# Two-layer hybrid attention trunk on one core: causal additions behind the sparse mask, block flips copied half by VectorE, two groups of turns side by side

## The chip, the cores and the metric

One NeuronCore of a Trainium2 chip runs the whole program. The metric is device time in microseconds (us). The kernel before took 1001.78 us in the median of 3 runs (1001.54 to 1001.94).

## What is computed

Two identical layers on x of 256 tokens by 1024 channels, all in float32. Each layer is half a SwiGLU feed-forward step (2816 hidden channels), a mixer, and half a feed-forward step again:

```python
h = h + 0.5 * swiglu(rms_norm(h), ffn1)
u = rms_norm(h); P = u @ w_in
# A: 4 heads, one shared key/value head; the 64 best keys per query by an 8-head ReLU indexer
# B: 4 heads, one block of 256, so plain causal attention here
# C: 8 heads, s + cumsum(log f)[q] - cumsum(log f)[k], output gated by a sigmoid
h = h + concat(o_A, o_B, o_C) @ w_out
h = h + 0.5 * swiglu(rms_norm(h), ffn2)
```

A and B have normed and rotated queries and keys, C normed ones. Logits above the diagonal are masked before the softmax.

## The kernel before

**Matrix products.** Each float32 weight is split into a high part (rounded by ScalarE, line 126) and a low part (the difference, taken by VectorE, line 130). TensorE multiplies high by high, high by low and low by high, so most of its work is products of 128x512 at line 340. The class `Weights` loads 1 MB pieces through SP's queue, five at a time, and splits them into units of 1024 columns up to seven ahead of their use; `pump` makes one high part and the low part of the unit before. `high` and `low` make one of the two alone.

**The mixer.** `mixer` goes through the columns of `w_in` in 8 chunks of 4 units. After each unit a counter `step` goes up by one (1 to 32), `run_side` emits the work that is due at that step by the numbers given to `at_step`, and one `pump` follows. A number of 28.5 is thus emitted after unit 29, 21.3 after unit 22. All engines run their instructions in the order in which they were emitted; an instruction whose input isn't ready holds up all behind it on its engine, and no other engine. So the table of step numbers sets when TensorE meets each group of small turns between its products, and nothing moves them at run time.

The pieces that the change and the prediction speak of, for each layer:

- `log_sigmoid` and `forget` make the forget logs `lf` (ScalarE, VectorE). `cumsum` turns them on TensorE (line 905, two turns) and sums them along the tokens on VectorE (line 907). `sums_out` writes the sums to DRAM, `sums_in` reads them back, spread over all partitions, into `first` (in the tile `tab`) and `later` (tiles `laterkT` and `laterlater`), 512 KB each, through SP's queue.
- `causal_part(0)` and `(1)` add the causal mask to `first` and the first `later` on GpSimd (line 932), so that the masks of the C heads are ready made. `causal_part(2)` and `(3)` do the second half on VectorE, later (`w2`, `w3` in `AC_ORDER`).
- `a_rope` rotates the sparse heads' queries `aqr` and key `ak` on GpSimd (steps 18 and 19). `a_norm` (number 21.3) sums the squares on VectorE (`ssa`), takes the roots on GpSimd (line 351) and scales the key into `akd` on GpSimd (line 720). `a_turn` (28.5) turns four blocks of `aqr` and two of `akd` on TensorE (line 970) and copies them out on ScalarE.
- GpSimd also has the roots and scalings of the C heads' keys (`y_ck`, `cka`), which stand ahead of `y_a` and `akd` in its order.
- `topk` finds the 64 best keys on VectorE (lines 883 and 884), and `amask` turns what is left into the sparse mask (line 895).
- At step 30 the text `EARLY` is emitted word by word: `S` flips the B heads' probabilities on TensorE (line 180), copies them out of PSUM (`spread`, by `turned`, line 193), and issues the A heads' scores and the B heads' values; `m` masks a head (line 1092), `e` takes its exponentials, `Q` and `q` make a high part, `j` a low part. Then units 31 and 32 follow on TensorE, and `AC_ORDER` is emitted.

PSUM has two rotating sets of four banks, `acc` and `gu`.

Of the kernel before, what the change touches and what calls it, by code (L numbers as in the profile page):

```python
# [10 lines left out]
F32 = mybir.dt.float32  # L11
# [3 lines left out]
ALU = mybir.AluOpType  # L15
# [3 lines left out]
P = 128  # L19
S = 256  # L20
# [6 lines left out]
TOPK = 64  # L27
# [10 lines left out]
WARM = 6  # L38
BRIDGE = 3
P_BUFS = 4  # L40
EARLY = "S Q q m0 e0 m1 e1 m2 e2 b0 b1 m3 j B0 B1 e3"
AC_ORDER = """
    h0 n0 d0 C n1 d1 d2 d3 T c0 F0 k0 F1 y0 y1 c1 k1 s2 v0 v1 m4 m5 g o0 o1 e4 e5 s3 s4
    h1 m6 m7 w2 e6 e7 l q q n2 n3 w3 m8 m9 h2 h3
# [1 line left out]
    r0 r1 n5 j F4 F5 y4 y5 h4 j v4 v5 o4 o5 j  # L46
    p h5 h6 h7 Z r2 N p r3 p r4 p M x2 p x3 p
"""
B_TURN, A_ROPE, B_STEP, A_ROOT, A_TURN, SUMS_STEP, TOP_STEP, A_STEP = 18, 18, 20, 21.3, 28.5, 21, 15, 30


CHUNKS = [
# [102 lines left out]
def kernel(ctx: ExitStack, tc: tile.TileContext, x, ffn1_norm, ffn1_w_gate, ffn1_w_up, ffn1_w_down,  # L155
# [10 lines left out]
    at = ctx.enter_context(tc.tile_pool(name="at", bufs=1))  # L166
# [5 lines left out]
    V, A, G, T = nc.vector, nc.scalar, nc.gpsimd, nc.tensor  # L172

    def bank(tag):
        return psum.tile([P, 512], F32, name="ps_" + tag, tag=tag)
# [6 lines left out]
    def turned(ps, dst, copies):  # L182
        for e, copy in enumerate(copies):
            d = dst[..., 64 * e:64 * e + 64]
            n = 64
            for k in d.shape[1:-1]:
                n *= k
            src = ps[e][:, :n]
            if len(d.shape) == 3:
                src = src.rearrange("p (b j) -> p b j", j=64)  # L190
            else:
                src = src.rearrange("p (a b j) -> p a b j", a=d.shape[1], j=64)
            copy(d, src)
# [4 lines left out]
    def tmp(n):  # L198
        return tp.tile([P, 512], F32, name="tmp", tag="tmp")[:, :n]
# [39 lines left out]
    W = Weights(tc, raw_pool, split_pool)  # L239
# [89 lines left out]
    causal = cp.tile([P, 3 * P], F32, name="causal")  # L329
# [12 lines left out]
    def mm3(o, lhs, rhs, start, stop):  # L342
        mm(o, lhs[0], rhs[0], start, False)
        mm(o, lhs[0], rhs[1], False, False)
        mm(o, lhs[1], rhs[0], False, stop)
# [344 lines left out]
    def mixer(l, norm, nxt):  # L690
        side, count = [], itertools.count()
        step = [0]

        def at_step(n, fn):
            side.append((n, next(count), fn))

        def run_side():
            due = sorted(x for x in side if x[0] <= step[0])
            for x in due:
                x[2]()  # L700
            side[:] = [x for x in side if x[0] > step[0]]
# [47 lines left out]
        st = {}  # L749
# [44 lines left out]
        def post_ib(ps):  # L794
# [10 lines left out]
            for t in range(2):  # L805
                x = small[t][:, None, 0:64]
# [24 lines left out]
                A.activation(la, la, AF.Ln, bias=1.0)  # L831
                A.activation(small[0][:, 0:1], ones[:, 0:1], AF.Exp)

            at_step(SUMS_STEP - 3, log_sigmoid)
            def forget():
                V.scalar_tensor_tensor(lf, fg, 0.0, la, op0=ALU.min, op1=ALU.subtract)

            at_step(SUMS_STEP - 2, forget)
            st["ikT"] = at.tile([P, 1, S], F32, name="ikT", tag="qs")

            def turn_ik():
# [42 lines left out]
                V.match_replace(out=st["score"][t], in_to_replace=m8, in_values=st["score"][t], imm_value=-3e38)  # L884

            def amask_begin():
                st["amask"] = at.tile([P, 3 * P], F32, name="amask", tag="amask")
                G.tensor_copy(st["amask"][:TOPK, 0:P], causal[:TOPK, 0:P])

            at_step(A_STEP - 4, amask_begin)  # L890

            def amask():
                am, score = st["amask"], st["score"]
                for d, x in ((am[:, P:], score[1]), (am[TOPK:, :P], score[0][TOPK:])):
                    V.tensor_scalar(d, x, -2e38, NEG, op0=ALU.is_gt, op1=ALU.mult)

            at_step(A_STEP - 0.5, amask)

            for r in range(TOPK // 8):
                at_step(TOP_STEP + 2 * r, lambda: topk(1))  # L900
# [20 lines left out]
                    nc.sync.dma_start(to, bass.AP(tensor=src.tensor, offset=src.offset + h * S,  # L921
                                                    ap=[[0, P], [S, k], [1, n]]))

            at_step(SUMS_STEP + 1, cumsum)
            at_step(SUMS_STEP + 3, sums_out)
            at_step(SUMS_STEP + 5, sums_in)
            for i in range(2):
                at_step(A_STEP - 2, lambda i=i: causal_part(i))

        def causal_part(i):  # L930
            x = st["first"][:, 2 * i:2 * i + 4] if i % 2 == 0 else st["later"][i // 2][:, :, 1]
            (V if i > 1 else G).tensor_tensor(x, x, causal[:, None, 0:P].to_broadcast([P, 4, P]), op=ALU.add)

        def post_a(ps):
            ss = sm.tile([P, 2, 5], F32, name="ssa", tag="ss")
# [116 lines left out]
        def tanh():  # L1052
            ps, hr = st.pop("cg"), st["hr"]
            sg = at.tile([P, 2, 512], F32, name="sg", tag="sg")
            for t in range(2):
                A.activation(sg[:, t], ps[t], AF.Tanh, scale=hr[:, t:t + 1])
            st["sg"] = sg
            for _ in range(2):
                bank("gu")


        def run_heads(hs, qk, emit=None):
            pj, pt, op, sums, bs, wide, flipped, gated, high = {}, {}, {}, {}, {}, {}, {}, {}, {}
            divided = range(2)
            blocks = ((slice(0, P), slice(0, P), slice(0, P)), (slice(P, 3 * P), slice(P, S), slice(0, S)))
            tag = "acc" if emit else "gu"
# [66 lines left out]
            def spread(p):  # L1133
                both = pp.tile([P, 8, P], F32, name="pT", tag="pT", bufs=2)
                kind, h = hs[2 * p]
                turned(flipped.pop(p), both[:, :6] if p in divided else both,
                       (A.copy if emit else V.tensor_copy, A.copy))
                pt[p] = [both[:, 3 * e:3 * e + 3].rearrange("p a b -> p (a b)") for e in range(2)]
                gated[p] = both[:, 6:8].rearrange("p a b -> p (a b)")
                if kind == "C":  # L1140
                    o = st["gate"][:, h // 2]
                    if p not in divided:
                        o = tmp(S)
                        G.tensor_tensor(o, gated[p], st["gate"][:, h // 2], op=ALU.mult)
                    gated[p] = o
# [36 lines left out]
            if emit is None:  # L1182
                return scores, masks, exps, roots, divide, flip, spread, values, outT
# [20 lines left out]
        def both_scores(_):  # L1204
# [8 lines left out]
            for p in range(2):  # L1213
                b_values(p, st["keys"][p][:, S:])

        todo = dict(S=both_scores, D=divide, d=lambda i: divide(i, V), s=scores, m=masks, e=exps, n=roots, F=flip, y=spread, v=values, o=outT,
                    Q=lambda _: W.high(), q=lambda _: W.high(), j=lambda _: W.low(),
                    b=lambda p: st["B"][1](p), B=lambda p: st["B"][2](p), T=lambda _: tanh(), w=causal_part)

        def do(text):  # L1220
            for word in text.split():
                todo[word[0]](int(word[1:] or 0))

        at_step(A_STEP, lambda: do(EARLY))

        oT = {}
        posts = dict(ib=post_ib, a=post_a, b=post_b, ck=post_ck, cq=post_cq, cv=post_cv, cg=post_cg)
        index_queries()
        for name, cols in CHUNKS[1:]:
            n = sum(c[1] for c in cols)  # L1230
            ps = [bank("gu") for _ in range(2)]
            for u in range(4):
                w = W.take()
                for kk in range(2):
                    k = 2 * u + kk
                    for t in range(2):
                        ts = slice(t * P, (t + 1) * P)
                        mm3(ps[t][:, :n], (norm.h[:, k, ts], norm.l[:, k, ts]), [v[:, kk] for v in w],
                            k == 0, k == KT - 1)
                step[0] += 1  # L1240
                run_side()
                if step[0] < A_STEP and step[0] != 8:
                    W.pump()
            posts[name](ps)
            if step[0] == 8:
                W.pump(2)
# [70 lines left out]
        def norm_out(_):  # L1317
# [5 lines left out]
            for t in range(2):  # L1323
# [3 lines left out]
                    p=lambda _: W.pump(), Z=residuals, N=norm_T, M=norm_out)  # L1327
# [23 lines left out]
    for l in range(DEPTH):  # L1351
        norm = ffn(norm, lambda: Norm(1, l), lambda: before_mixer(l), l == 0)
        norm = mixer(l, norm, lambda: Norm(2, l))
        norm = ffn(norm, (lambda: Norm(0, l + 1)) if l + 1 < DEPTH else None)
# [37 lines left out]
```

## Time and profile before

| | |
|---|---|
| median of 3 runs | 1001.78 us |
| the profiled execution | 1001.55 us |
| its span | 999.8 us |
| TensorE (PE) busy | 995.5 us, 100% of the span |
| its weight loads (PEld) | 856.5 us, 86% |
| VectorE (DVE) busy | 799.3 us, 80% |
| ScalarE (ACT) busy | 597.4 us, 60% |
| GpSimd (POOL) busy | 162.0 us, 16% |
| mean granted TensorE clock | 0.999 |

The span runs from the first to the last instruction; the time of a run is 1.75 us longer than the span in this execution. TensorE's instructions overlap in the profile, and their ends are modelled: what a product costs is read from the distance between the starts of two that follow each other. The two mixers lie at about 208 to 318 us and 703 to 813 us.

### The profile page before, as it was taken

How to read it: one execution, taken by the hardware profiler on the slowest of the kernel's cores; microseconds unless marked ns; L12 is line 12 of the kernel's file. 1: busy time of each engine (PE TensorE's matmuls, PEld its weight loads, DVE VectorE, ACT ScalarE, POOL GpSimd, SP SyncE). 2: the span in 40 equal slices, each digit the busy share in tenths (PEclk: the TensorE clock that was granted, in tenths of full speed). 3: DMA queues.
4: the chain of work that ended last, by engine and by line, in shares of the span. 5: the costliest groups of instructions: out<-in, count | busy, mean ns of one | idle time of the engine just before them, and what ended most of it. 6: DMA issues, size and time to landing. Idle time of an engine off the chain costs nothing.

```text
span 999.8 us, 15219 instructions
## 1 busy us (share of the span) xinstructions
PE 995.5 (100%) x5692; PEld 856.5 (86%) x5692; DVE 799.3 (80%) x1482; ACT 597.4 (60%) x1118; POOL 162.0 (16%) x188
## 2 busy tenths in 40 slices
PE   9999999999999999999999999999999999999998
PEld 8888888888878888888888888889888788888887
DVE  5978778789998777777888777787899977777775
ACT  6655555597786555555465555556968765555552
POOL 2003000058812000000000020001677210000000
PEclk9999999999999999999999999999999999999999
DMA  9865647475725555555655655565566164464731
GB/s 291 274 224 160 224 156 238 129 238 188 230 87 169 173 164 193 187 195 196 199 169 176 207 183 198 185 208 166 192 211 232 58 208 159 140 238 148 232 128 43
DMA packets 133498, 184.80 MB, mean 185 GB/s; under 512 B 7152, under 2 KB 106800, under 8 KB 133424
## 3 DMA queue, kind: packets, MB, share of 16 engines
q1 hardware_dynamic: 133392, 183.82, 56.2%
q8 instruction: 45, 0.74, 0.3%
q14 instruction: 29, 0.24, 0.1%
q10 hardware_dynamic: 32, 0.01, 0.0%
HBM read 182.75 MB, written 1.06 MB: 184 GB/s over the span
## 4 chain that ended last, share of the span: by engine, by line
PE 98%; DMA 1%; SPq 0%; ACT 0%; issue 0%; DVE 0%
PE ps_gu L340 66%; PE ps_acc L340 30%; PE ps_acc L180 1%; DMA raw<-in_ffn_w_up_dram 1%; PE ps_acc L375 1%; PE ps_gu L180 1%; SPq L100 0%; SPq L225 0%; PE ps_gu L375 0%; PE ps_acc L970 0%; ACT wh L126 0%; PE ps_acc L402 0%; PE ps_acc L844 0%; PE ps_acc L905 0%; DVE trunk L419 0%
## 5 line engine op out<-in xcount | busy, mean ns | idle before, releaser
L130 DVE TENSOR_TENSOR wl<-raw,wh 128x1024 fp32r<-128x1024 f32 (+2 forms) x342 | 421.6, 1240 | 27.1 <-ACT wh L126 27.1
L126 ACT CAST wh<-raw 128x1024 fp32r<-128x1024 f32 (+2 forms) x341 | 341.2, 1037 | 14.4 <-PE ps_acc L340 7.7
L340 PE MATMUL ps_gu<-xhl,wh 128*128 128x512 f32 (+1 forms) x1472 | 347.6, 388 | 0.2 <-ACT wh L126 0.2
L340 PEld LDWEIGHTS ps_gu<-xhl,wh 128*128 128x128 f32 x1472 | 272.5, 188 | 54.4 <-ACT wh L126 0.7
L340 PEld LDWEIGHTS ps_gu<-xhl,wl 128*128 128x128 f32 x1472 | 187.5, 191 | 4.1 <-DVE wl L521 0.2
L340 PE MATMUL ps_gu<-xhl,wl 128*128 128x256 f32 (+1 forms) x1472 | 190.3, 282 | 0.0
L484 DVE TENSOR_TENSOR tmp<-ps_gu,tmp 128x256 f32<-128x256 f32 x176 | 72.8, 422 | 109.3 <-ACT tmp L483 109.0
L340 PE MATMUL ps_acc<-wh,hh 128*128 128x512 f32 (+1 forms) x352 | 137.3, 390 | 0.0
L340 PE MATMUL ps_acc<-wl,hh 128*128 128x512 f32 (+1 forms) x352 | 137.0, 389 | 0.0
L340 PE MATMUL ps_acc<-wh,hl 128*128 128x512 f32 (+1 forms) x352 | 136.6, 388 | 0.0
L340 PE MATMUL ps_gu<-wh,xhl 128*128 128x512 f32 (+2 forms) x448 | 133.4, 375 | 0.0
L483 ACT COPY tmp<-ps_gu 128x256 f32<-128x256 f32 x176 | 63.4, 371 | 92.1 <-PE ps_gu L340 91.9
L498 ACT CAST hh<-tmp 128x256 fp32r<-128x256 f32 x80 | 32.6, 407 | 120.2 <-DVE tmp L495 120.2
L340 PEld LDWEIGHTS ps_gu<-wh,xhl 128*128 128x128 f32 x448 | 82.5, 188 | 14.1 <-issue 1.7
L490 ACT ACTIVATE tmp<-tmp 128x256 f32<-128x256 f32 x88 | 36.9, 419 | 82.7 <-DVE tmp L488 82.5
L340 PE MATMUL ps_gu<-wl,xhl 128*128 128x512 f32 (+2 forms) x224 | 83.2, 372 | 0.0
L351 POOL TENSOR_TENSOR y_n<-msq,minus_half 128x2 f32<-128x2 f32 x6 | 7.0, 1174 | 441.9 <-DVE msq L350 441.9
L340 PEld LDWEIGHTS ps_acc<-wh,hl 128*128 128x128 f32 x352 | 66.1, 188 | 13.9
L340 PEld LDWEIGHTS ps_acc<-wh,hh 128*128 128x128 f32 x352 | 66.2, 188 | 12.6
L340 PEld LDWEIGHTS ps_acc<-wl,hh 128*128 128x128 f32 x352 | 66.3, 188 | 12.3 <-DVE wl L130 0.2
L340 PEld LDWEIGHTS ps_gu<-wl,xhl 128*128 128x128 f32 x224 | 42.2, 188 | 5.9
L508 DVE TENSOR_TENSOR tmp<-tmp,rb 128x256 f32<-128x256 f32 x88 | 37.7, 428 | 3.0
(237 smaller groups left out, 901.5 us busy)
## 6 DMA issues: line engine op xcount, KB each, us to landing
raw<-in_ffn_w_down_dram SPq DMA_DIRECT2D x44, 1024.0 KB, 5.0
raw<-in_ffn_w_gate_dram SPq DMA_DIRECT2D x42, 1024.0 KB, 6.9
raw<-in_ffn_w_up_dram SPq DMA_DIRECT2D x42, 1024.0 KB, 7.8
raw<-in_w_in_dram SPq DMA_DIRECT2D x24, 1024.0 KB, 5.1
raw<-in_w_out_dram SPq DMA_DIRECT2D x8, 1024.0 KB, 5.0
raw<-in_w_in_dram SPq DMA_DIRECT2D x4, 768.0 KB, 5.0
raw<-in_w_in_dram SPq DMA_DIRECT2D x4, 656.0 KB, 4.2
raw<-in_ffn_w_gate_dram SPq DMA_DIRECT2D x3, 512.0 KB, 7.5
```

Source lines behind the costliest of these rows:

```text
L126: self.nc.scalar.copy(hv, src)
L130: (engine or self.nc.vector).tensor_tensor(lv, self.srcs[self.n_low], hv.bitcast(F32), op=ALU.subtract)
L180: T.transpose(b[:, 64 * i:64 * i + 64], src[r], ident[r, r])
L340: T.matmul(o, l, r, start=start, stop=stop, skip_group_check=True)
L351: G.tensor_tensor(y, dst, minus_half[:, :n], op=ALU.pow)
L375: T.transpose(ps[:, i, t * P:(t + 1) * P], trunk[:, t, (2 * mp + i) * P:(2 * mp + i + 1) * P], ident)
L483: A.copy(o, ps[:, 1])
L484: V.tensor_tensor(o, ps[:, 0], o, op=ALU.add)
L490: A.activation(th, t_, AF.Tanh, scale=0.5)
L498: (V.tensor_copy if late else A.copy)(hh, t_)
L508: V.tensor_tensor(t_, t_, norm.rb, op=ALU.mult)
```

## The change

Six edits, the same in both layers:

1. `A_TURN` goes from 28.5 to 24, and `SUMS_STEP` from 21 to 24 with `cumsum` at `SUMS_STEP` in place of one after it. The turns of the forget logs go from step 22 to 24, those of the sparse heads from 29 to 24, right behind them. The forget logs themselves stay at steps 18 and 19.
2. `sums_out` goes from step 24 to 26, `sums_in` from 26 to 27.
3. The mask `amask` is not emitted ahead of `EARLY` any more; it is a word `a` in it, behind `S` and a low part `j`.
4. At step 29 only a high part is made; its low part is that `j`, behind `S`.
5. `amask` has one more block of 128 columns, into which VectorE copies the causal mask behind the sparse mask. GpSimd's `causal_part(0)` and `(1)` are emitted behind it and read this block in place of `causal`.
6. `spread` copies the B heads' flips half by VectorE and half by ScalarE, in place of all by ScalarE.

```diff
-EARLY = "S Q q m0 e0 m1 e1 m2 e2 b0 b1 m3 j B0 B1 e3"
+EARLY = "S j a Q q m0 e0 m1 e1 m2 e2 b0 b1 m3 j B0 B1 e3"
...
-B_TURN, A_ROPE, B_STEP, A_ROOT, A_TURN, SUMS_STEP, TOP_STEP, A_STEP = 18, 18, 20, 21.3, 28.5, 21, 15, 30
+B_TURN, A_ROPE, B_STEP, A_ROOT, A_TURN, SUMS_STEP, TOP_STEP, A_STEP = 18, 18, 20, 21.3, 24, 24, 15, 30
...
-            at_step(SUMS_STEP - 3, log_sigmoid)
+            at_step(18, log_sigmoid)
...
-            at_step(SUMS_STEP - 2, forget)
+            at_step(19, forget)
...
-                st["amask"] = at.tile([P, 3 * P], F32, name="amask", tag="amask")
+                st["amask"] = at.tile([P, 4 * P], F32, name="amask", tag="amask")
...
-                for d, x in ((am[:, P:], score[1]), (am[TOPK:, :P], score[0][TOPK:])):
+                for d, x in ((am[:, P:3 * P], score[1]), (am[TOPK:, :P], score[0][TOPK:])):
                     V.tensor_scalar(d, x, -2e38, NEG, op0=ALU.is_gt, op1=ALU.mult)
-
-            at_step(A_STEP - 0.5, amask)
+                V.tensor_copy(am[:, 3 * P:], causal[:, 0:P])
+                for i in range(2):
+                    causal_part(i)
+
+            st["mask"] = amask
...
-            at_step(SUMS_STEP + 1, cumsum)
-            at_step(SUMS_STEP + 3, sums_out)
-            at_step(SUMS_STEP + 5, sums_in)
-            for i in range(2):
-                at_step(A_STEP - 2, lambda i=i: causal_part(i))
+            at_step(SUMS_STEP, cumsum)
+            at_step(SUMS_STEP + 2, sums_out)
+            at_step(SUMS_STEP + 3, sums_in)
...
-            (V if i > 1 else G).tensor_tensor(x, x, causal[:, None, 0:P].to_broadcast([P, 4, P]), op=ALU.add)
+            late = i > 1
+            mask = causal[:, 0:P] if late else st["amask"][:, 3 * P:]
+            (V if late else G).tensor_tensor(x, x, mask[:, None].to_broadcast([P, 4, P]), op=ALU.add)
...
-                       (A.copy if emit else V.tensor_copy, A.copy))
+                       (V.tensor_copy, A.copy))
...
-                if step[0] < A_STEP and step[0] != 8:
+                if step[0] < A_STEP - 1 and step[0] != 8:
                     W.pump()
+                if step[0] == A_STEP - 1:
+                    W.high()
```

On TensorE, in the first layer's mixer of the kernel before, the turns of the forget logs (`lf`) stand between units 22 and 23, and 84 products later those of the sparse heads between units 29 and 30:

```order
L340 MATMUL ps_gu<-wh,xhl 128x512
L905 MATMUL ps_acc<-ident,lf 8x128 x2
L340 MATMUL ps_gu<-wh,xhl 128x512
...
L340 MATMUL ps_gu<-wh,xhl 128x512
L970 MATMUL ps_acc<-ident,aqr 128x128 x4
L970 MATMUL ps_acc<-ident,akd_2514 128x128
L970 MATMUL ps_acc<-ident,akd_2515 128x128
L340 MATMUL ps_gu<-wh,xhl 128x512
```

In the changed kernel both stand together between units 24 and 25:

```order
L340 MATMUL ps_gu<-wh,xhl 128x512
L908 MATMUL ps_acc<-ident,lf 8x128 x2
L973 MATMUL ps_acc<-ident,aqr 128x128 x4
L973 MATMUL ps_acc<-ident,akd_2514 128x128
L973 MATMUL ps_acc<-ident,akd_2515 128x128
L340 MATMUL ps_gu<-wh,xhl 128x512
```

The forget logs' turns moved back by 24 products, the sparse heads' forward by 60. GpSimd's instructions up to `akd` stand in the same order in both kernels.

On VectorE, at step 30 of the first layer, the kernel before has the last low part (line 130) between the last round of `topk` and the mask:

```order
L884 MATCH_REPLACE score_2339<-m_2979,score_2339 128x256
L130 TENSOR_TENSOR wl<-raw,wh 128x1024
L895 TENSOR_SCALAR amask<-score_2339 128x256
L895 TENSOR_SCALAR amask<-score_2338 64x128
L1092 ISA tmp,nm<-ps_acc,amask,minus_a 128x128
```

and the changed kernel:

```order
L884 MATCH_REPLACE score_2339<-m_2977,score_2339 128x256
L193 COPY pT<-ps_acc 128x6x64 x2
L130 TENSOR_TENSOR wl<-raw,wh 128x1024
L895 TENSOR_SCALAR amask<-score_2339 128x256
L895 TENSOR_SCALAR amask<-score_2338 64x128
L896 COPY amask<-causal 128x128
L1095 ISA tmp,nm<-ps_acc,amask,minus_a 128x128
```

Two copies of the flips went ahead of the low part, and one copy of the causal mask went behind the sparse mask.

On SP's queue the three reads of the sums stood ahead of the first piece of the next feed-forward step's weights and now stand behind it:

```order
 L100 DMA raw<-in_w_in_dram 128x4x512 x8
-L100 DMA raw<-in_w_out_dram 128x2x1024 x3
-L911 DMA sums_of<-tmp 8x256
-L100 DMA raw<-in_w_out_dram 128x2x1024
-L921 DMA tab<-sums_of 128x8x128
-L921 DMA laterkT<-sums_of 128x1024
-L921 DMA laterlater<-sums_of 128x1024
+L100 DMA raw<-in_w_out_dram 128x2x1024 x4
+L914 DMA sums_of<-tmp 8x256
 L100 DMA raw<-in_ffn_w_gate_dram 128x8x256
+L924 DMA tab<-sums_of 128x8x128
+L924 DMA laterkT<-sums_of 128x1024
+L924 DMA laterlater<-sums_of 128x1024
```

The write of the sums now stands behind the last piece of `w_out`.

## Rows read from the trace of the kernel before

**Rows 1.** The page, busy time and share of the span, with instructions.

```profile
PE 995.5 (100%) x5692; PEld 856.5 (86%) x5692; DVE 799.3 (80%) x1482; ACT 597.4 (60%) x1118; POOL 162.0 (16%) x188
```

**Rows 2.** Waits of PE over the whole span: us in total, times, longest.

```profile
PE ps_gu L340 <- POOL minus_half L219: 1.0, 1, 1.0
PE ps_gu L340 <- ACT wh L126: 0.2, 1, 0.2
```

**Rows 3.** Timeline of PE, first mixer, steps 22 to 24: start, length, engine, what.

```profile
250.34 0.38 PE L905 MATMUL ps_acc<-ident,lf 128*8 128x128 f32 x2
250.47 0.48 PE L340 MATMUL ps_gu<-wh,xhl 128*128 128x512 f32 x1
250.79 0.39 PE L340 MATMUL ps_gu<-wl,xhl 128*128 128x512 f32 x1
...
255.80 0.61 PE L340 MATMUL ps_gu<-wh,xhl 128*128 128x512 f32 x2
```

**Rows 4.** Timeline of PE, first mixer, the sparse heads' turns at step 29.

```profile
269.63 0.60 PE L970 MATMUL ps_acc<-ident,aqr 128*128 128x128 f32 x4
270.07 0.38 PE L970 MATMUL ps_acc<-ident,akd 128*128 128x128 f32 x2
270.20 0.48 PE L340 MATMUL ps_gu<-wh,xhl 128*128 128x512 f32 x1
```

**Rows 5.** Timeline of POOL, first mixer, up to the sparse heads' key.

```profile
251.16 2.91 POOL L351 TENSOR_TENSOR y_ck<-c_ss,minus_half 128x16 f32<-128x16 f32 x1 [4.68 <-DVE c_ss L350]
...
256.20 1.95 POOL L351 TENSOR_TENSOR y_a<-ssa,minus_half 128x10 f32<-128x10 f32 x1
258.23 0.76 POOL L720 TENSOR_TENSOR akd<-ak,y_a 128x128 f32<-128x128 f32 x2
```

**Rows 6.** Timeline of DVE, first mixer, the sparse heads' sums of squares.

```profile
255.16 0.17 DVE L350 TENSOR_SCALAR ssa<-ssa 128x10 f32<-128x10 f32 x1
```

**Rows 7.** Timelines of PE and of POOL, second mixer, the same places.

```profile
745.37 0.48 PE L340 MATMUL ps_gu<-wh,xhl 128*128 128x512 f32 x1
...
753.13 0.76 POOL L720 TENSOR_TENSOR akd<-ak,y_a 128x128 f32<-128x128 f32 x2
```

**Rows 8.** Timelines of POOL, DVE, ACT and PE, first mixer, around step 30.

```profile
273.58 1.26 POOL L932 TENSOR_TENSOR tab<-tab,causal 128x512 f32<-128x512 f32 x1
...
273.85 3.32 DVE L130 TENSOR_TENSOR wl<-raw,wh 128x1024 fp32r<-128x1024 f32 x1
277.09 0.52 DVE L895 TENSOR_SCALAR amask<-score 128x256 f32<-128x256 f32 x2
280.50 1.22 DVE L130 TENSOR_TENSOR wl<-raw,wh 128x1024 fp32r<-128x1024 f32 x1
285.28 1.02 DVE L193 COPY pT<-ps_gu 128x384 f32<-128x384 f32 x2
...
275.84 1.52 PE L340 MATMUL ps_acc<-pT,vB 128*64 128x256 f32 x16
```

**Rows 9.** DMA issues (us to landing), SP's timeline, DVE's first C-head mask, first mixer.

```profile
laterlater<-sums_of SPq DMA_DIRECT2D x1, 512.0 KB, 8.1
...
268.53 0.38 SPq L100 DMA_DIRECT2D raw<-in_ffn_w_gate_dram  x1
...
286.98 0.29 DVE L1092 CUSTOM_DVE_ANT_0 tmp<-ps_gu,tab 128x128 f32<-128x128 f32 x1
```

**Rows 10.** Timeline of PE, start and end of the span; windows of the end.

```profile
1.05 2.93 PE L340 MATMUL ps_gu<-ones 128*128 128x128 f32 x12 [1.05 <-POOL minus_half L219]
4.12 1.11 PE L537 MATMUL ps_acc<-ident,trunk 128*128 128x128 f32 x4
7.50 0.60 PE L537 MATMUL ps_acc<-ident,trunk 128*128 128x128 f32 x4
996.47 0.28 PE L340 MATMUL ps_gu<-wh,hl 128*128 128x256 f32 x1
998.00:999.80 1.80, 0.00 (x0) 0.00 (x0) 0.00 (x0) 0.00 (x0) 0.00 (x0) 0.71 0.21 73
```

More of the change, by code (lines that the diff above doesn't have):

```diff
@@ L1217, in mixer @@
                     Q=lambda _: W.high(), q=lambda _: W.high(), j=lambda _: W.low(),
-                    b=lambda p: st["B"][1](p), B=lambda p: st["B"][2](p), T=lambda _: tanh(), w=causal_part)
+                    b=lambda p: st["B"][1](p), B=lambda p: st["B"][2](p), T=lambda _: tanh(), w=causal_part,
+                    a=lambda _: st["mask"]())
         def do(text):
```

## The prediction

> **What bounds the kernel now.** I read the page first: TensorE is busy for 995.5 of 999.8 us [rows 1]. The waits of PE come next: the longest is 1.0 us at the start of the program, and the other is 0.2 us [rows 2]. So no wait of a mixer is there to be removed. Busy time of overlapping products could hide small waits, so I looked at the starts. From the product that starts at 250.79 to the one at 255.80 there are 22 steps [rows 3], 5.01 / 22 = 0.228 us each, and I take the other stretches of wide products as the same. TensorE runs at its own pace through both mixers, and the kernel gets faster only by less work on TensorE. It gets slower by whatever makes TensorE wait, to the full amount, since nothing later has slack to give it back.
>
> The Trainium skill judges TensorE's headroom otherwise: Perfetto Trace Analysis, "Identifying the Most-Contended Engine", calls matmul busy time a bad measure and asks for the busy share of weight loads. That share is 86% here [rows 1], which by the rule leaves headroom, and rival 4's 999.4 us is what it could give; the even starts above say that this headroom is no waiting time, and the measurement decides.
>
> **Part 1: the turns side by side.** This is the edit that touches TensorE's order.
>
> What it saves: a group of turns between wide products costs its own time and a slower first product behind it. The forget logs' group takes 250.47 - 250.34 = 0.13 us, and the product behind it holds its place for 250.79 - 250.47 = 0.32 us in place of 0.23 [rows 3]: 0.22 us in all. The two turns themselves stay, so joining the groups saves some 0.1 us a layer.
>
> What it adds: the sparse heads' turns need `akd` from GpSimd, and they move forward past 60 products. Where does TensorE get there?
> - Behind the old stop the first product starts at 250.47, the second at 250.79, and the 24th at 255.80 [rows 3]. Unit 25's first would start at 256.03.
> - The stop at step 22 is gone, so all this comes 0.22 earlier: the forget logs' turns start at 255.81, and take 0.13.
> - The four turns of `aqr` take 270.07 - 269.63 = 0.44 [rows 4]. So TensorE asks for `akd` at 255.81 + 0.13 + 0.44 = 256.38.
>
> When is `akd` there? GpSimd gets its sums of squares from VectorE at 255.16 + 0.17 = 255.33 [rows 6], but it is still with the C heads' keys, which it began at 251.16 after waiting for VectorE, and takes the root only at 256.20. The two scalings run from 258.23 to 258.99 [rows 5]. None of what comes before on GpSimd or VectorE is moved by the change, and VectorE's order up to these sums is the same. So TensorE waits 258.99 - 256.38 = 2.6 us. In the kernel before the same turns came at 269.63, 11 us behind `akd`; that cover is what the new place gives up.
>
> Sum of one layer: I allow 0.08 us for the hand-over, as between the end of `y_a` at 258.15 and the scaling that reads it [rows 5], and 0.07 for the last `akd` turn. Unit 25 then starts at 258.99 + 0.08 + 0.07 = 259.14, 3.1 us later than before. The old stop at step 29 is not paid any more, 270.20 - 269.63 = 0.57 [rows 4]; the slower product behind a stop is paid once in both kernels, there or here. So 3.1 - 0.57 = 2.5 us. In the second mixer the product behind the old stop starts at 745.37, unit 25 would start at 750.93, and the scalings end at 753.13 + 0.76 = 753.89 [rows 7], 2.96 behind it, just as 258.99 is behind 256.03. So twice 2.5: **+5.0 us**. Bounds of one layer: 1.7 and 3.3, the 0.76 of the scalings to either side, since the scan of the sums that VectorE did beside them moves away and a low part takes its place.
>
> **Part 2: the clock.** A wait of 2.6 us has no like inside this trace. The nearest is the end: the last product starts at 996.47 and lasts 0.28, and the window from 998.00 to 999.80 has a granted clock of 0.71 [rows 10]. With levels of 1 and 0.5 this means a fall to 1.2 GHz about 0.76 us into the window, at 998.8, 2.0 us after TensorE's last work. The forecast wait is longer than these 2.0. The price is seen at the start: four turns took 1.11 us at 4.12 and 0.60 at 7.50 [rows 10], so TensorE, working from 1.05 on, was at half pace for at least 3.1 and at most 6.5 us, and lost half of it, 1.5 to 3.2. I take 1.6 for a fall, near the lower end: at the start the engine also waited between its pieces, and here wide products follow at once. One example of a fall doesn't tell whether each wait of this length brings one. I take it that one of the two layers has it: **+1.6 us**. Bounds: 0 and twice 3.2.
>
> A rule speaks against this term. The Trainium skill (TensorE: Matmul & The Clock Gate, "Why this matters for your kernels") bids to avoid only longer idle gaps than the one that I forecast, so by it the clock stays at 2.4 GHz and the time is 1006.8 us. No row here shows such a gap with work behind it. It is the first rival below.
>
> **Part 3: the rest, at nothing.**
> - GpSimd's additions behind the mask. Before, they ran from 273.58 on, 1.26 us each, and a low part on VectorE that began at 273.85 took 3.32 us where another took 1.22 [rows 8]. Some 2 us of VectorE come free. TensorE doesn't wait for VectorE there [rows 2], so the gain is spent on idle time. In their new place they run beside the sparse heads' masks; if they block VectorE again it costs as much as before. First use is at 286.98 [rows 9], 9.9 us behind the mask at 277.09.
> - The copies of the flips. VectorE pays 1.02 us for two [rows 8] and ScalarE pays as many less. TensorE's values of the B heads start at 275.84 [rows 8] and need all four. VectorE was through with its selection at 273.85, so its two end by about 274.9, 0.9 us ahead, and with TensorE 2.5 us later there is more. If that cover is gone, the cost is at most 1.0 us a layer.
> - The copy of the causal mask: at most half of the 0.52 us that VectorE takes for the two pieces of the sparse mask [rows 8], 0.26 us, which the 2 us that come free cover.
> - The low part behind `S`: the same instruction, some 1 us later. Units are split several ahead of their use, 12 products or 12 x 0.228 = 2.7 us of TensorE each, so nothing waits.
> - SP's queue: the write of the sums moves behind one weight piece, the reads behind another that was issued at 268.53; the reads took up to 8.1 us to land [rows 9]. Behind it they land by 268.9 + 8.1 = 277.0, and by 285.1 if the piece's own transfer delays them by as much again, ahead of the masks at 286.98. The weight pieces get ahead of the reads, so no weight comes later.
>
> **Sum.** Of the profiled execution: 1001.55 + 5.0 + 1.6 = 1008.15. The median of the runs stands 0.23 us above it, so I predict 1008.4 us.
>
> **The rivals.**
> 1. The wait without a fall of the clock: 1001.78 + 5.0 = 1006.8. For it: one example of a fall is little, and it came with no work behind it. Against it: that example needed only 2.0 us.
> 2. A fall in both layers: 1006.8 + 3.2 = 1010.0. For it: both waits are of one length. Against it: the same doubt.
> 3. `akd` is there in time, so only the joining counts: 1001.78 - 2 x 0.1 = 1001.6, not slower. It decides from the point at which GpSimd ends `akd` 2.6 us earlier. For it speaks only that the C heads' keys waited 4.68 us for VectorE [rows 5]; against it, nothing in the change makes VectorE earlier there.
> 4. VectorE held TensorE in a way that the waits don't show, and its 2 us a layer free TensorE: the 2.1 us less the 1.0 of the copies, twice, give 1001.6 - 2.2 = 999.4, if there is also no wait for `akd`. Against it are the even starts [rows 3].
> 5. A longer wait, because GpSimd's order is disturbed or PSUM's next bank is still read by VectorE's mask of a B head: 1 us more a layer, 1010.4 with a fall in one.
>
> **How the numbers follow.** Wait with one fall 0.40, without 0.27, with two 0.20, longer 0.06; `akd` in time 0.05, VectorE freed 0.02. The range reaches from the case without a fall, with its wait 0.5 us a layer shorter, to the case with two falls, with 0.2 us a layer more: 1005.8 to 1010.4. It leaves out rivals 3 and 4 and the outer part of the bounds. A measurement of this kernel can tell about 0.2%, 2 us, from no change. Slower by more than that: 0.93. Within it: 0.05. Faster: 0.02.
>
> **What would show it.** Right: in the waits of PE, two of about 2.6 us at the turns of `akd`, on GpSimd's scaling; a granted clock below 1 in the window behind one of them, with wide products 0.45 apart; VectorE's low part at step 30 back at 1.2 us. Part 1 is wrong if TensorE goes through these turns without a wait, or for another input; part 2 if the clock stays at 1, or falls in both layers. Part 3 is wrong if TensorE waits for a flip's copy, a mask or a low part behind step 30. The whole is wrong if the time is under 1004.

## The result, and the profile after

The changed kernel took 1008.75 us in the median of 6 runs (1007.76 to 1009.7), against 1001.7 of the kernel before on the same chip (1001.05 to 1001.94): a ratio of 1.0071, with a 95% interval of 1.0058 to 1.0084. It is slower by 7 us, where 6.6 were forecast.

The profiled execution took 1008.14 us, its span 1006.4, its clock 0.998. Busy times and waits of PE, to hold against [rows 1, 2]; first the page:

```profile
PE 997.3 (99%) x5692; PEld 857.8 (85%) x5692; DVE 797.6 (79%) x1488; ACT 596.3 (59%) x1114; POOL 162.4 (16%) x188
```

Then the waits of PE over the span (us in total, times, longest):

```profile
PE ps_acc L973 <- POOL akd L720: 4.5, 2, 2.4
PE ps_gu L340 <- POOL minus_half L219: 1.0, 1, 1.0
PE ps_gu L340 <- ACT wh L126: 0.4, 1, 0.4
```

One line is new: two waits, 4.5 us together, for the sparse heads' key. The busy time tells nearly nothing: it grew by 1.8 us, and most of the loss is no busy time at all.

How the span's 6.6 us divide is read from starts. I take a mixer from the first product of its first chunk to the last product of its output projection, and what lies between the two mixers and behind them separately. In us:

| | before | after | difference |
|---|---|---|---|
| first mixer | 126.39 | 128.66 | +2.27 |
| second mixer | 126.39 | 130.52 | +4.13 |
| between the mixers | 368.51 | 368.51 | 0 |
| behind the second | 183.50 | 183.50 | 0 |

The lengths are distances between starts. The first and the last product of the first mixer, before:

```profile
191.67 0.51 PE L340 MATMUL ps_gu<-xhl,wh 128*128 128x384 f32 x2
318.07 0.39 PE L340 MATMUL ps_acc<-wh,ohl 128*128 128x512 f32 x1
```

and after:

```profile
191.88 0.51 PE L340 MATMUL ps_gu<-xhl,wh 128*128 128x384 f32 x2
320.54 0.39 PE L340 MATMUL ps_acc<-wh,ohl 128*128 128x512 f32 x1
```

The second mixer of the kernel before goes from 686.57 to 812.97 in the same way, so by this measure both begin some 16 us earlier than the 208 and 703 us named further up.

The other 0.2 us are at the program's start, ahead of anything that was changed. All the rest is in the mixers, and they differ by 1.9 us although the edits are the same in both. The timeline of PE shows the turns of the first mixer (start, length, what, and the wait in brackets), to hold against [rows 3, 4]:

```profile
255.96 0.38 PE L908 MATMUL ps_acc<-ident,lf 128*8 128x128 f32 x2
256.17 0.60 PE L973 MATMUL ps_acc<-ident,aqr 128*128 128x128 f32 x4
258.89 0.68 PE L973 MATMUL ps_acc<-ident,akd 128*128 128x128 f32 x2 [2.12 <-POOL akd L720]
259.33 0.48 PE L340 MATMUL ps_gu<-wh,xhl 128*128 128x512 f32 x1
...
261.26 0.61 PE L340 MATMUL ps_gu<-wh,xhl 128*128 128x512 f32 x2
```

and those of the second:

```profile
756.32 0.77 PE L973 MATMUL ps_acc<-ident,akd 128*128 128x128 f32 x2 [2.38 <-POOL akd L720]
756.76 0.75 PE L340 MATMUL ps_gu<-wh,xhl 128*128 128x512 f32 x1
...
760.27 0.63 PE L340 MATMUL ps_gu<-wh,xhl 128*128 128x512 f32 x2
```

From unit 25's first product to its ninth, TensorE takes 261.26 - 259.33 = 1.93 us in the first mixer and 760.27 - 756.76 = 3.51 in the second. The same products cost 1.58 us more, and the windows of the second mixer say why. Their columns are the stretch, its length, busy time and instructions of PE, PEld, DVE, ACT and POOL, the granted clock, the DMA share and GB/s:

```profile
755.00:757.00 2.00, 0.65 (x3) 0.46 (x4) 1.93 (x8) 2.00 (x8) 1.78 (x4) 0.95 0.34 43
757.00:759.00 2.00, 2.00 (x6) 1.54 (x6) 1.66 (x5) 2.00 (x6) 1.42 (x1) 0.50 0.83 326
759.00:761.00 2.00, 2.00 (x8) 1.58 (x7) 2.00 (x4) 2.00 (x4) 2.00 (x2) 0.70 0.38 156
```

TensorE idles in the first of them, and in the next the clock is at 0.50: 1.2 GHz, while wide products are waiting to go through. In the first mixer's windows over the same wait and behind it the clock is 1.00:

```profile
258.00:260.00 2.00, 1.08 (x5) 0.80 (x6) 1.62 (x9) 2.00 (x10) 1.34 (x4) 1.00 0.38 47
260.00:262.00 2.00, 2.00 (x11) 1.63 (x10) 1.97 (x6) 2.00 (x4) 1.84 (x2) 1.00 0.98 401
```

So this execution has one fall in two layers. The six runs lie in two groups, three at 1007.76 to 1008.26 with a mean clock of 0.998 and three at 1009.23 to 1009.7 with 0.996 or 0.997. The groups are about 1.4 us apart, as one fall more would make them; the other five runs left no windows to read, so their falls are inferred from that.

GpSimd in the first mixer, to hold against [rows 5], shows that the key came no earlier than before:

```profile
251.37 2.91 POOL L351 TENSOR_TENSOR y_ck<-c_ss,minus_half 128x16 f32<-128x16 f32 x1 [4.68 <-DVE c_ss L350]
...
256.41 1.95 POOL L351 TENSOR_TENSOR y_a<-ssa,minus_half 128x10 f32<-128x10 f32 x1
258.44 0.76 POOL L720 TENSOR_TENSOR akd<-ak,y_a 128x128 f32<-128x128 f32 x2
```

Each stands 0.21 us behind its row of before, the shift of the program's start. In the second mixer `y_ck` starts at 748.80 and the scalings at 755.87, 497.43 us later than in the first. TensorE's products there lie 494.90 us apart in the kernel before (750.93 to 256.03), and 2.27 more here, which is 497.17. So the key is 0.26 us later against them, and the wait is 2.38 in place of 2.12.

At step 30 the timeline of DVE shows the other edits doing what they say, against [rows 8]:

```profile
276.48 1.02 DVE L193 COPY pT<-ps_acc 128x384 f32<-128x384 f32 x2 [1.88 <-PE ps_acc L180]
277.42 1.22 DVE L130 TENSOR_TENSOR wl<-raw,wh 128x1024 fp32r<-128x1024 f32 x1
278.55 0.53 DVE L895 TENSOR_SCALAR amask<-score 128x256 f32<-128x256 f32 x2
279.11 0.23 DVE L896 COPY amask<-causal 128x128 f32<-128x128 f32 x1
```

The low part takes 1.22 us in place of 3.32. GpSimd's additions run from 279.42 on, beside the masks. VectorE, however, stood idle for 1.88 us ahead of its copies, waiting for flips that TensorE's own stall had made late: the time won on VectorE meets a TensorE that isn't there yet.

The Trainium skill (SBUF — State Buffer, "SBUF: two separate sides") says that VectorE and GpSimd share a pair of ports which one of them locks for a whole instruction; VectorE takes it for an operation with two inputs in SBUF, against a GpSimd operation that reads there. The trace agrees: a low part, two inputs from SBUF, took 3.32 us beside the additions and 1.22 without them.

### The profile page after: what moved, and what is told of

The parts are those of the page before. It is cut to its first block, busy times and chain, and to the rows that moved or that the text cites. A ratio compares the mean times of both kernels' runs of the same rounds, so it can differ in the third digit from the quotient of the medians.

```text
span 1006.4 us, 15223 instructions
## 1 busy us (share of the span) xinstructions
PE 997.3 (99%) x5692; PEld 857.8 (85%) x5692; DVE 797.6 (79%) x1488; ACT 596.3 (59%) x1114; POOL 162.4 (16%) x188
## 4 chain that ended last, share of the span: by engine, by line
PE 90%; POOL 4%; issue 2%; DVE 2%; DMA 1%; ACT 1%; SPq 0%; DVEq 0%; POOLq 0%; ACTq 0%
PE ps_gu L340 59%; PE ps_acc L340 29%; DMA raw<-in_ffn_w_up_dram 1%; PE ps_acc L375 1%; DVE score L870 1%; PE ps_acc L180 1%; DVE wl L130 1%; POOL y_ck L351 1%; POOL y_bk L351 1%; POOL aqr L714 1%; PE ps_gu L180 1%; ACT wh L126 0%; POOL swapped L712 0%; POOL bkr L720 0%; POOL aqr L715 0%
```

## The experiments

My theory after the result: the key's wait and the clock that falls behind it make all of the loss; the edits at step 30 make none and win none. The rivals: the edits at step 30 cost something too; the new place of the forget logs does; or a wait alone doesn't make the clock fall. Each of the four kernels that follow changes one part.

**e1: the sparse heads' turns put back.** The changed kernel with one number.

```diff
-B_TURN, A_ROPE, B_STEP, A_ROOT, A_TURN, SUMS_STEP, TOP_STEP, A_STEP = 18, 18, 20, 21.3, 24, 24, 15, 30
+B_TURN, A_ROPE, B_STEP, A_ROOT, A_TURN, SUMS_STEP, TOP_STEP, A_STEP = 18, 18, 20, 21.3, 28.5, 24, 15, 30
```

> The changed kernel with the sparse heads' turns alone put back to 28.5. Theory (all of the loss is the wait for akd at step 24, with the clock's fall behind it): no wait of PE on GpSimd's scaling, granted clock 1, within 0.5 us of the kernel before, 1001.2 to 1002.2. Rival (the edits at step 30, or the forget logs' turns at step 24, have a share): some us stay, over 1003.

Measured: 1002.29 us (1001.84 to 1002.72), ratio 1.0007 [0.9998, 1.0015], clock 1. One number out of six edits takes back over 6 of the 7 us. Of all edits, moving `A_TURN` is the one that costs. The time is 0.1 us above the range that was expected. Against the kernel before, its mixers are 0.14 and 0.38 us longer, and its waits of PE show a first sign of the reason:

```profile
PE ps_acc L340 <- DVE pT L193: 0.2, 1, 0.2
```

A product of step 30 waits for VectorE's copy of a flip, which Part 3 had named as the sign that it is wrong.

**e2: the sparse heads' turns forward, and nothing else.** The kernel before with one number.

```diff
-B_TURN, A_ROPE, B_STEP, A_ROOT, A_TURN, SUMS_STEP, TOP_STEP, A_STEP = 18, 18, 20, 21.3, 28.5, 21, 15, 30
+B_TURN, A_ROPE, B_STEP, A_ROOT, A_TURN, SUMS_STEP, TOP_STEP, A_STEP = 18, 18, 20, 21.3, 24, 21, 15, 30
```

> The kernel before with the sparse heads' turns alone put forward to 24; forget logs at 22, step 30 as before. Theory: two waits of about 2.3 us for akd and a fall of the clock in one or both layers, 1007 to 1010.5, as the changed kernel. Rival (the loss needs the two groups side by side, or the edits at step 30): under 1004.

Measured: 1009.52 us (1008.1 to 1010.02), ratio 1.0076 [1.0063, 1.0088]. This edit alone makes the whole loss. Its waits of PE, then its windows behind each:

```profile
PE ps_acc L970 <- POOL akd L720: 4.1, 2, 2.1
```

```profile
260.00:262.00 2.00, 2.00 (x7) 1.52 (x6) 1.97 (x5) 2.00 (x4) 1.96 (x2) 0.50 0.92 358
759.00:761.00 2.00, 2.00 (x6) 1.53 (x5) 1.97 (x5) 2.00 (x4) 2.00 (x2) 0.50 0.98 375
```

Here both mixers have the fall, and both are longer by nearly the same, 4.08 and 3.94 us. The waits are 2.06 and 2.05 us long, shorter than the 2.12 of the changed kernel's first mixer, which brought no fall. So the length of the wait doesn't decide it by itself.

**e3: the key made earlier.** The changed kernel with GpSimd's root of the sparse heads a unit ahead.

```diff
-B_TURN, A_ROPE, B_STEP, A_ROOT, A_TURN, SUMS_STEP, TOP_STEP, A_STEP = 18, 18, 20, 21.3, 24, 24, 15, 30
+B_TURN, A_ROPE, B_STEP, A_ROOT, A_TURN, SUMS_STEP, TOP_STEP, A_STEP = 18, 18, 20, 20.2, 24, 24, 15, 30
```

> The changed kernel with the sparse heads' norm one step earlier (number 20.2 in place of 21.3), so that GpSimd takes y_a and akd ahead of the C heads' keys; the turns stay side by side at 24. Theory: akd is ready about 253.5, PE doesn't wait, clock 1, and the joining saves 0.1 us a layer: 1001.2 to 1001.8. Rival (the group at this place costs by itself, by its size or by a PSUM bank that VectorE still reads): over 1004, and PE waits there for another input.

Measured: 1002.1 us (1001.75 to 1002.48), ratio 1.0004 [0.9996, 1.0013]. The turns stay where the change put them; only their input comes earlier. GpSimd's row, and PE's:

```profile
253.19 0.76 POOL L720 TENSOR_TENSOR akd<-ak,y_a 128x128 f32<-128x128 f32 x2
...
256.80 0.38 PE L973 MATMUL ps_acc<-ident,akd 128*128 128x128 f32 x2
```

The key is done at 253.95 and asked for at 256.80, the wait is gone, the clock stays at 1, and the loss is gone too. So it isn't the place of the turns that costs, but their input. It missed its expectation from above by 0.3 us, for the reason that e1 hinted at: its mixers are 0.14 and 0.42 us longer than before's, not shorter.

**e4: the edits at step 30 alone.** The kernel before with the new `EARLY`, the mask's block and the halved copies, while the turns, the sums and their reads stay at their old steps.

```diff
-EARLY = "S Q q m0 e0 m1 e1 m2 e2 b0 b1 m3 j B0 B1 e3"
+EARLY = "S j a Q q m0 e0 m1 e1 m2 e2 b0 b1 m3 j B0 B1 e3"
...
-                       (A.copy if emit else V.tensor_copy, A.copy))
+                       (V.tensor_copy, A.copy))
```

> The kernel before with only the edits at step 30: the mask and a low part behind S, GpSimd's additions behind the mask, flips copied half by VectorE. Theory: VectorE's low part there goes from 3.3 to 1.2 us, and the time stays within 0.3 us of before, since TensorE never waited for it. Rival (freed VectorE gives TensorE time): 999.4 to 1001. Other rival (VectorE's copies are late for the B heads' values): 1002.5 to 1004.

Measured: 1001.86 us (1001.63 to 1002.22), ratio 1.0002 [0.9993, 1.0011]. No gain and no loss that can be told. VectorE's low part takes 1.22 us here too, and freeing VectorE of 2 us a layer is worth nothing in the time. The trace has two small sides to it. At step 30 each layer gains 0.2 us (below), and the first mixer loses some 0.7 to a wait of a product of the output projection for GpSimd's `ohl`, so that it ends 0.5 longer and the second mixer 0.3 shorter:

```profile
307.44 0.73 PE L340 MATMUL ps_acc<-wh,ohl 128*128 128x512 f32 x2 [0.47 <-POOL ohl L1183]
```

Then I asked how a wait of another length behaves, with the same place made harmless first.

**e5: the turns one unit later.** The changed kernel with both groups at step 25.

```diff
-B_TURN, A_ROPE, B_STEP, A_ROOT, A_TURN, SUMS_STEP, TOP_STEP, A_STEP = 18, 18, 20, 21.3, 24, 24, 15, 30
+B_TURN, A_ROPE, B_STEP, A_ROOT, A_TURN, SUMS_STEP, TOP_STEP, A_STEP = 18, 18, 20, 21.3, 25, 25, 15, 30
```

> The changed kernel with both groups of turns one unit later (A_TURN and SUMS_STEP 25). Theory: TensorE asks for akd 2.7 us later, about when it is ready, so the wait goes to under 0.3 us, the clock stays at 1, and 1001.5 to 1002.5 is left. Rival (the place behind a chunk's last unit, or the joined group, costs by itself): over 1004.

Measured: 1002.64 us (1002.38 to 1003.41), against 1002.13 of the kernel before on this chip; ratio 1.0006 [0.9997, 1.0014]. That is 0.1 us above the range that was expected. No wait for the key: it is done at 258.77 + 0.76 = 259.53, and its turn starts at 259.66. The forecast's arithmetic of when TensorE arrives and when the key is there thus holds to some 0.1 us: 12 products later, 2.7 us, are just enough. A unit makes the difference between 7 us and none.

**e6 and e7: longer waits put in.** e5 with the key scaled three times, or six, in place of once; the result is the same.

```diff
-                for t in range(2):
-                    scale_heads(akd[t], ak[t], rs[:, 5 * t + 4:5 * t + 5])
+                for _ in range(3):
+                    for t in range(2):
+                        scale_heads(akd[t], ak[t], rs[:, 5 * t + 4:5 * t + 5])
```

> As the kernel with both groups one unit later, and GpSimd scales akd three times over (the same values each time, 1.5 us more ahead of the turns). It does more work than is needed, and leaves none out. Theory: two waits of about 1.5 us, each costing its own length; a wait this short leaves the clock at 1, so 1004.0 to 1005.3 with runs close together. Rival (any wait of a microsecond or more brings falls of the clock): 1006 to 1008.5 with runs spread by 1.6 us steps.

> As the kernel with both groups one unit later, and GpSimd scales akd six times over (the same values, 3.8 us more). Theory: two waits of about 3.8 us and a fall of the clock in both layers, each 1.6 to 1.7 us: 1001.8 + 7.6 + 3.3 = 1012.7, runs within 1 us of each other. Rival (the falls behind the changed kernel's waits are no matter of the wait's length): 1009.4 in some runs, spread over 3 us.

Measured: e6 1008.49 us (1006.62 to 1010.08), ratio 1.0061 [1.0049, 1.0074]; e7 1016.5 us (1016.08 to 1017.26), ratio 1.0144 [1.013, 1.0158]. Both are over what was expected: e6 by 3 us over its wait alone, and e7 by 4.

First, the dose was wrong. Two scalings took 0.76 us; six took 3.17 and twelve 6.32, more than three and six times as much. The last two of e6's first mixer on GpSimd, then VectorE beside them, show where the rest comes from:

```profile
259.71 1.74 POOL L720 TENSOR_TENSOR akd<-ak,y_a 128x128 f32<-128x128 f32 x2
259.82 1.37 DVE L130 TENSOR_TENSOR wl<-raw,wh 128x1024 fp32r<-128x1024 f32 x1
```

Each scaling takes 0.40 us, but the one that begins at 260.07, while a low part runs on VectorE, takes 1.38 and ends behind the low part. In e7 two of the twelve in each mixer take 1.38 to 1.41, and each of them begins inside a low part. So a low part held GpSimd up here, as GpSimd's additions held one up in the kernel before, and the second of e6's two waits comes from it.

But e6 also fell outside by its kind. Its timeline of PE in the second mixer:

```profile
757.28 0.33 PE L974 MATMUL ps_acc<-ident,akd 128*128 128x128 f32 x1 [1.09 <-POOL akd L720]
758.61 0.33 PE L974 MATMUL ps_acc<-ident,akd 128*128 128x128 f32 x1 [1.01 <-POOL akd L720]
```

and its windows there:

```profile
758.00:760.00 2.00, 1.39 (x5) 1.15 (x6) 1.97 (x6) 2.00 (x4) 2.00 (x3) 0.76 0.64 256
760.00:762.00 2.00, 2.00 (x7) 1.52 (x6) 1.93 (x9) 2.00 (x5) 2.00 (x4) 0.50 0.30 88
```

No wait is longer than 1.09 us, and yet the clock falls: two waits with one turn between them did it. In the first mixer of the same execution two such waits, 0.80 and 1.01, did not, and one of the five runs, of 1006.62 us, has a mean clock of 1. Against e5 the mixers are 1.81 and 3.40 us longer.

In e7 the waits are 4.97 and 5.24 us, and the clock falls in both mixers. Its windows, first mixer:

```profile
262.00:264.00 2.00, 0.00 (x0) 0.00 (x0) 1.97 (x5) 2.00 (x5) 2.00 (x4) 0.69 0.14 55
264.00:266.00 2.00, 1.50 (x5) 1.13 (x6) 1.97 (x6) 1.18 (x4) 2.00 (x6) 0.50 0.66 221
266.00:268.00 2.00, 2.00 (x6) 1.61 (x5) 1.93 (x6) 1.63 (x2) 2.00 (x2) 0.50 0.74 303
268.00:270.00 2.00, 2.00 (x7) 1.53 (x7) 1.97 (x5) 0.00 (x0) 2.00 (x2) 0.61 0.00 0
```

The fall begins while TensorE still waits, at 0.69, so part of it costs nothing. Against e5 the mixers are 7.15 and 6.84 us longer.

What a fall costs can't be had by taking the waits off these differences: e5 copies its flips late at step 30, as e3 does (the table of e8), with stretches of 2.94 and 3.08 us, where e6 and e7 need 2.50. It is read from starts instead, from the first product behind the turns to the 25th, two units on. In us:

| kernel, mixer | first | 25th | between | over e5 |
|---|---|---|---|---|
| e5, first | 259.80 | 265.35 | 5.56 | |
| after, first | 259.33 | 264.89 | 5.56 | 0 |
| after, second | 756.76 | 763.91 | 7.15 | 1.59 |
| e2, first | 259.09 | 266.22 | 7.13 | 1.57 |
| e2, second | 758.08 | 765.05 | 6.97 | 1.41 |
| e6, first | 261.59 | 267.15 | 5.56 | 0 |
| e6, second | 758.70 | 765.88 | 7.18 | 1.62 |
| e7, first | 264.99 | 272.67 | 7.68 | 2.12 |
| e7, second | 767.46 | 774.84 | 7.38 | 1.82 |

Behind waits more than twice as long, a fall is dearer by 0.2 to 0.7 us. The runs of e7 also lie within 1.2 us, where those of e2 and e6 spread over 1.9 and 3.5: a wait of 5 us brings a fall in each layer, as far as the runs can tell, and waits of about 2 us bring one sometimes.

**e8: the key earlier, and ScalarE making all copies of the flips again.** e3 with one line of `spread` as before.

```diff
-                       (V.tensor_copy, A.copy))
+                       (A.copy if emit else V.tensor_copy, A.copy))
```

> The changed kernel with the sparse heads' norm one step earlier (20.2), and the B heads' flips copied by ScalarE alone again. Theory (with the norm moved, the time over the kernel before came from VectorE's late copies of the flips, whose PSUM banks the A heads' second scores wait for): those waits of PE go, 1001.2 to 1001.7, 0.4 to 0.8 us under the kernel with VectorE's copies. Rival (the time over comes from somewhere else): 1002.0 to 1002.4 as that one.

Measured: 1002.25 us (1001.71 to 1002.79), against 1002.13 of the kernel before on this chip; ratio 1.0000 [0.9991, 1.0009]. By the time alone the rival's range holds and not the theory's; but this chip runs the kernel before 0.4 us slower than that of e3, and the trace decides. Its mixers are 126.36 and 126.36 us long in the trace, e3's 126.53 and 126.81, the kernel before's 126.39. So the halved copies are what made e3's mixers longer; but a third of a microsecond is less than the time itself can show. A start-up wait on the first loads was longer in this execution, so its span is no proof either.

The stretch from the flips to the values of the B heads at step 30 shows how. In us, from rows of PE and DVE like those above:

| kernel, mixer | flips start | VectorE's first copy | behind | values start | stretch |
|---|---|---|---|---|---|
| e4, first | 273.25 | 273.95 | 0.70 | 275.75 | 2.50 |
| e4, second | 768.64 | 769.35 | 0.71 | 771.14 | 2.50 |
| after, first | 275.86 | 276.48 | 0.62 | 278.36 | 2.50 |
| e1, first | 273.00 | 274.16 | 1.16 | 275.86 | 2.86 |
| e3, first | 273.47 | 274.70 | 1.23 | 276.40 | 2.93 |
| e3, second | 768.63 | 770.02 | 1.39 | 771.71 | 3.08 |
| e1, second | 768.01 | 769.46 | 1.45 | 771.15 | 3.14 |

With ScalarE alone, in the kernel before, the stretch is 275.84 - 273.15 = 2.69 us. With both engines it is 2.50 where VectorE's copy follows in 0.7, and 1.69 or 1.70 plus its lateness where it comes later. From 1.0 behind, the sharing loses. VectorE is at the end of its selection there, so it comes when that is through. Two rows of e1, PE and then DVE, show it:

```profile
768.01 0.96 PE L180 MATMUL ps_acc<-ident,p 64*128 64x64 f32 x24
...
770.06 0.70 PE L340 MATMUL ps_acc<-aT 64*128 64x128 f32 x5 [0.16 <-DVE pT L193]
```

```profile
769.46 1.01 DVE L193 COPY pT<-ps_acc 128x384 f32<-128x384 f32 x2
```

It isn't the values that wait first but the A heads' second scores, which need the PSUM bank that the copy empties.

**e9: a version meant to win.** e4, with the sparse heads' turns at step 22 beside the forget logs' old place, and the root of the key still earlier, so that the key is there.

```diff
-B_TURN, A_ROPE, B_STEP, A_ROOT, A_TURN, SUMS_STEP, TOP_STEP, A_STEP = 18, 18, 20, 21.3, 28.5, 21, 15, 30
+B_TURN, A_ROPE, B_STEP, A_ROOT, A_TURN, SUMS_STEP, TOP_STEP, A_STEP = 18, 18, 20, 19.5, 22, 21, 15, 30
```

> The edits at step 30, the forget logs where the kernel before has them, and the sparse heads' turns joined to them at step 22, with the sparse heads' norm at 19.5 so that GpSimd takes y_a and akd ahead of the C heads' keys. Theory: akd is ready about 250, a microsecond before TensorE asks for it; no wait, clock 1, and each mixer some 0.3 us shorter than before (0.1 by the joining, 0.2 by the step-30 edits with VectorE in time): 1001.0 to 1001.6, hard to tell from before. Rival (VectorE's copies of the flips are late again): 1001.9 to 1002.4. Other rival (akd still late): over 1003.

Measured: 1017.11 us (1015.18 to 1017.39), ratio 1.0152 [1.0138, 1.0166]. It is the slowest of all, 15 us above what was expected. Its key was done at 251.01 + 0.76 = 251.77. That is 0.8 late for turns that TensorE would have reached at 250.34 + 0.21 + 0.44 = 250.99, but it isn't what held them. The waits of PE name another engine:

```profile
PE ps_acc L973 <- DVE nm L1095: 9.4, 4, 2.8
```

and its timeline shows it in the first mixer, PE and then DVE:

```profile
253.55 1.09 PE L973 MATMUL ps_acc<-ident,aqr 128*128 128x128 f32 x4 [2.83 <-DVE nm L1095]
256.29 0.66 PE L973 MATMUL ps_acc<-ident,akd 128*128 128x128 f32 x2 [1.65 <-DVE nm L1095]
```

```profile
252.91 0.48 DVE L1095 CUSTOM_DVE_ANT_0 tmp<-ps_acc,causal,minus_b 128x256 f32<-128x256 f32 x1
...
255.65 0.48 DVE L1095 CUSTOM_DVE_ANT_0 tmp<-ps_acc,causal,minus_b 128x256 f32<-128x256 f32 x1
```

Each group of turns starts a little behind a mask of a B head: the turns write to banks of `acc` in which VectorE still reads scores. The queries' turns had their input in time, and their output was not free. Two units later, in the changed kernel, the turns show no such wait. About 1 us of the first wait goes back to the early root, whose sums VectorE now takes ahead of this mask: the mask ends at 253.39 here and at 252.43 in e4. The four waits are 9.4 of the 13.6 us that the two mixers are longer than before. With them the clock falls in both mixers; a window in the midst of the first one's waits:

```profile
254.00:256.00 2.00, 0.64 (x4) 0.24 (x2) 2.00 (x6) 0.52 (x3) 1.92 (x2) 0.50 0.53 215
```

No version beats the kernel before by anything that can be measured.

## Why the prediction was right

**What bounds the kernel** held. TensorE goes from product to product, and each wait that was put in came out in the time in full: 2.27 us of the first mixer are one wait and what belongs to it, with nothing given back until the end of the program. The other half of it held in e4 too: 2 us freed on VectorE bought nothing.

**Part 1** was right in place, cause and size. Unit 25 started 259.33 - 256.03 - 0.21 = 3.09 us later in the first mixer, for a forecast of 3.1; less the 0.57 of the old stop, 2.52 for 2.5. In the second mixer it is 3.35 less 0.57, 2.78, because GpSimd got to the C heads' keys 0.26 us later there, and all behind them with it; I had carried over the first mixer's figure, and that was within the bounds. Together 5.3 for 5.0. The wait as the view of waits lists it, 2.12, is shorter than the 2.6 that were forecast, for two reasons. That view counts from the modelled end of the turns before, 256.17 + 0.60 = 256.77, and only up to the first of the key's two turns, at 258.89. The second waits for a scaling of its own, so that the two take 259.33 - 258.89 = 0.44 us in place of 0.13 [rows 4]. Starts are what the sum is to be read from. The point of its rival 3, a key 2.6 us earlier, was tried from both sides: e3's key came over 5 us earlier and e5's turns 2.7 later, and both have no wait.

**Part 2** was right in kind, and the count of one was luck. The fall cost 1.58 us, for 1.6; that it came so close is in part luck too, as 1.6 was picked near the lower end of 1.5 to 3.2, and the falls of all kernels cost 1.4 to 2.1. The profiled execution has one, and half of the runs have a time that fits two; e2, with the shorter waits, had two where it was profiled. Rivals 1 and 2 are thus no other theories but other throws of the same chance, except that no profile of the kernel with this wait shows none. The rule behind rival 1 is refuted for this kernel: the Trainium skill (TensorE: Matmul & The Clock Gate, "Why this matters for your kernels") bids to avoid only longer gaps than these, and here the clock was at 0.50 behind waits of 2.38, of 2.06, and of 1.09 and 1.01 with a turn between. What makes one wait of 2 us bring a fall and another not stays open. Neither its length nor its place alone decides, and nothing tried here varied what TensorE did ahead of it.

**Part 3** was right in the time and wrong in one of its steps. The step: the copies of the flips cost nothing since VectorE's two end 0.9 us ahead of the B heads' values. The values are not the first to wait; the A heads' second scores are, for a PSUM bank, as in the table of e8. The term was 0.2 us a layer to the good in the changed kernel, because TensorE's own stall had made VectorE early. In the kernels without the stall and with the sums at the later step (e1, e3) VectorE comes late, and it is 0.2 to 0.45 to the bad. The mask, the low part behind `S` and the reads of the sums cost nothing, as said: TensorE waits for none of them.

The sum by parts is 5.3 + 1.6 - 0.4 = 6.5, for 6.40 in the mixers. That Part 1's 0.3 too little and Part 3's 0.4 too much nearly cancel is chance. The forecast's 6.6 was a little under the median's 7.05, as half of the runs, by their times, have the second fall.

**Rival 4** fell with e4, where VectorE was freed of the 2 us a layer and TensorE gained nothing in the time. **Rival 5** named the right neighbour: its PSUM bank isn't what held step 24, but two units earlier it is (e9).

## What to carry to other kernels

When an engine that bounds a kernel is given work at an earlier place, ask two questions there: when is the input made, and by whom, and when is the bank free that it writes to. The one held this change up and the other e9, and a unit of distance made the difference between 7 us and none. A wait put into a TensorE that is otherwise always busy should be priced with a fall of the clock behind it, and a helper's share of the work counts only if the helper is there when it is asked for.

## What was not expected

- Two waits of about 1 us, with one turn between, brought the clock down as one of 2 did (e6), and in the first mixer of the same run they did not.
- A fall cost 1.4 to 1.6 us behind waits of about 2 us and 1.8 to 2.1 behind waits of 5, so that it weighs most beside short waits.
- A GpSimd scaling of 0.40 us took 1.38 where it began inside a low part on VectorE (e6), so that the wait put in through GpSimd came out longer than planned by way of VectorE.
